# A hybrid attention layer on one core: two stores in place of four for each projected q and k, and a reordered preparation of the output projection's weights

## The chip, the cores and the metric

The kernel runs on one core of one Trainium2 chip. Its time is device time in microseconds for one execution of the whole layer; the figure quoted is the median of three runs. The core has a matrix engine (TensorE; PE in the profile, its weight loads PEld), three other compute engines (VectorE = DVE, ScalarE = ACT, GpSimd = POOL) and SyncE (SP), whose queue here issues nearly all transfers between the on-chip memory and DRAM (DMAs). Each engine works through its own instructions in order; semaphores hold an engine until what it needs from another is there.

## The reference

One layer, 1024 positions, width 1024, float32. All matrices are dense.

```python
h = x @ w_in                                    # 1024 x 5120
qa, ka, va, qb, kb, vb, ga, gb = split(h)       # 8 + 8 heads of 64, two gates of 1024
y_a = chunk_band_attention(qa, ka, va, rel_bias) @ w_proj_a     # softmax, band of 9 chunks of 64
y_b = stick_breaking_attention(qb, kb, vb) @ w_proj_b           # causal, cumulative log sums
mix = (sigmoid(ga + b) * y_a + sigmoid(gb + b) * y_b) @ w_out
x = layer_norm(alpha * x + mix, g1, b1)
g, u = split(x @ w_ffn_in)                      # 2 x 2816
x = layer_norm(alpha * x + (silu(g) * u) @ w_ffn_out, g2, b2)
```

## The kernel before

**Numbers and products.** Every operand of a matmul is split in two rounded halves: `split(hi, lo, src)` casts on ScalarE (hi) and subtracts on VectorE (lo = src - hi). A product is then three matmuls (hi·hi, hi·lo, lo·hi). Most big products use seven block products instead of eight (a Strassen-like scheme, numbered p1 to p7 and run in the order 1, 2, 6, 5, 7 or 3, ...); their weights and inputs are sums of blocks, made on VectorE beforehand. One block product is 12 matmuls of 128x512 in the input projection and in the feed-forward part, 24 in the output projection.

**Stages, in order of time.** (1) Input projection. The list `work` has entries 0 to 13: entry 0 is a pair of q and k columns made with plain products, entries 1 to 4 and 6 to 8 are further pairs of q and k by seven products, entry 5 is v, entries 9 to 13 are gates. `run_pairs` drives them; `left(i)` and `right(i)` load and split the weights of entry i (tiles wLp, wRp; the split sums are wlp, wbp, wap, wcp, here with the entry's number behind them: wap1 belongs to entry 1). Results are gathered in tiles called c, one for q and one for k: ScalarE copies a block product out of PSUM or VectorE adds it. `out_qk` then splits c into hi and lo, and `store_hl` stores both to DRAM (`q_dr`, `k_dr`), from which the heads load them later. An aside of this stage (`sum_wo`) makes sums of the blocks of `w_out` and stores them (`wt_dr`); another stores the split weights of the branch projections (`wp_dr`). (2) Eight softmax heads (tiles with _a), then eight stick-breaking heads (_b), with gate products and branch A's projection between them. (3) Branch B's projection: eight column blocks c, each two accumulators `yBps`, whose results are multiplied by the gate tile gB and added to the stored other branch (`mA`). (4) The output projection. Rows 0 to 511 use seven products, `ops` p1 to p7, with weight tiles "11", "21", "22" and the sums "t1" to "t4" (raw wr_o/wr_ot, halves wh_ and wl_); rows 512 to 1023 use plain products in a last loop over `hf` and `tt` with "11", "21", "12", "22". `take_in` adds a finished accumulator to the residual tile `acc`; `layer_norm` follows per 128 rows. (5) Feed-forward up and down, second layer norm.

**Slots and banks.** On-chip tiles come from rings of slots of 128x1024 floats by tag:

```python
SLOTS = dict(bw=9, pt=4, yt=3, qs=2, kh=2, kl=2, v=2, gt=3, kp=4, op=8, xt=16)
BANKS = dict(mm=2, sc=2, tr=3, pv=1)
```

In stage 1 the tiles c, hi and lo of the q/k pairs, the output tiles of v (vc) and the tiles of `sum_wo` and `store_proj` take turns in the eight slots of `QKV = ("qs", "kh", "kl", "v")` (`cycle`); entry 0's halves and some others use `("qs", "kl")` only. A new tile waits until the last reader of its slot is done; for a tile that was stored, that is the landing of its store. PSUM accumulators likewise come in rings of 2, 2, 3 and 1 banks.

**What sets the order.** The framework schedules instructions by itself; `tc.keep_in_program_order(ins)` ties an instruction to the order in which the code is written. SP's queue issues DMAs in its own order, and an issue waits there until its source is ready and its destination free; all that stands behind it on SP waits too. Eight DMA semaphores take turns, so a DMA also waits for the one issued eight places earlier on its semaphore to land.

**The part of the change.** `begin_w(srcs, name, raw, hl, lo_eng)` loads a weight tile and returns `end`, which makes its halves, the lower one on the engine `lo_eng`. Before, `begin_wo` gives GpSimd for "11", "21", "t1" to "t4" and VectorE for "22" and "12". A weight tile is begun when the one before has been ended, one or two products ahead of its use.

Of the kernel before, what the change touches and what calls it, by code (L numbers as in the profile page):

```python
# [11 lines left out]
F32 = mybir.dt.float32  # L12
# [6 lines left out]
P = 128  # L19
# [29 lines left out]
def hybrid_trunk_kernel(ctx: ExitStack, tc, x, xt, w_first, w_v, w_in, b_gate, rel_bias, w_proj,  # L49
# [272 lines left out]
    def small_inputs():  # L322

        rel_sb = cycle(QKV, "rel_sb")[0:8, 0:896]
        rel_in = cycle(QKV, "rel_in")[0:8, 0:N_REL]
        dma(rel_in, rel_bias)
        nc.vector.tensor_copy(rel_sb[:, 383:896], rel_in[:, ::-1])
        nc.vector.tensor_copy(rel_sb[:, 0:383], rel_in[:, 512:513].to_broadcast([8, 383]))
        dma(rel_dr, rel_sb)
        dma(bg, b_gate)  # L330

    def store_hl(d, hi, lo):
        for h in range(2):
            rows = slice(h * DH, (h + 1) * DH)
            dma(d[h * P:h * P + DH], hi[rows].bitcast(F32))
            dma(d[h * P + DH:(h + 1) * P], lo[rows])

    def project_plain(i):

# [162 lines left out]
    def aside_work(i):  # L502
        if i == 2:
            small_inputs()
        if i >= len(work) - 9:
            store_proj(i - len(work) + 9)
        if i in (5, 8):
            sum_wo(i // 6)

    def run_pairs(steps, left, right, also=lambda i: None, first=2, aside=lambda i: None,  # L510
                  then=lambda: None, wide=None, then_right=None):
# [24 lines left out]
            also(i)  # L536


    def begin_w(srcs, name, raw, hl, lo_eng):
        r = raw(f"wr_{name}")  # L540
        srcs = srcs if isinstance(srcs, list) else [(slice(0, 1024), srcs)]
        for cs, src in srcs:
            dma(r[:, cs], src)

        def end(tied=False):
            hi = hl(f"wh_{name}", F32R)
            lo = hl(f"wl_{name}", F32R)
            for ins in (nc.scalar.copy(hi, r),
                        lo_eng.tensor_tensor(lo, r, hi.bitcast(F32), ALU.subtract)):
# [419 lines left out]
    for hd in heads:  # L969
        for g in range(2):  # L970
# [7 lines left out]
            for st in range(8 - 4 * g):  # L978
                vsteps.append((hd, g, st, box))

    wi = 0
    pend = []
    steps_of = {}
# [6 lines left out]
    for si, (hd, g, st, box) in enumerate(vsteps):  # L990
        hidx, pos = si // nhead, si % nhead
        if hidx < 14 and pos == 8:
            load_qk(heads[hidx + 2])
            if hidx < 6:
                later.append([3, heads[hidx + 2]["end_bias"]])
        if pos == 4:
            if hidx < 15:
                load_v(heads[hidx + 1])
            else:
                next_w = begin_proj(1, 3)()  # L1000
        early = hd["br"] == 0 and st == LAG - 1 and len(pend) == LAG
# [70 lines left out]
    wo, m_raw = {}, {}  # L1072

    def begin_wo(name, raw, tag, lo_eng):
        ends = [begin_w((wt_dr if name in wt_dr else wo_src)[name][j], f"o{name}_{j}", of(raw),
                        of(tag), lo_eng) for j in range(2)]

        def end():
            wo[name] = [end_j() for end_j in ends]
        return end  # L1080

    def wo_op(name, kt):
        cs = (LO, HI)[kt % 2]
        return tuple(t[:, cs] for t in wo[name][kt // 2])

    for n, c in enumerate((6, 7, 5, 4, 0, 1, 2, 3)):
        if n % 2 == 0:
            w = next_w
            if n < 6:
                next_w = begin_proj(1, (2, 0, 1)[n // 2])()  # L1090
        gB = slot("kp", f"gB{c}")
        dma(gB, g_dr[2 * c + 1])
        squash(gB, c, 1)
        if c in kept:
            mA = kept[c]
        else:
            mA = slot("op", f"mA{c}")
            dma(mA, m_dr[c])
        for hf, cs in enumerate((LO, HI)):
            acc = bank("sc", f"yBps{c}_{hf}")  # L1100
            mm3(acc, [(w[0][:, ks], w[1][:, ks], yh[4 + k][:, cs], yl[4 + k][:, cs])
                      for k, ks in ((k, slice((c % 2) * HW + k * P, (c % 2) * HW + (k + 1) * P))
                                    for k in range(4))])
            nc.vector.tensor_tensor(gB[:, cs], acc, gB[:, cs], ALU.mult)
            nc.vector.tensor_tensor(mA[:, cs], gB[:, cs], mA[:, cs], ALU.add)
        m_raw[c] = mA
        t = m_high[c] = cycle(QKV, f"mo{c}", F32R)
        split(t[:, LO], t[:, HI], mA[:, HI])
        if c < 4:
            m_sums(c, m_raw[c + 4], mA)  # L1110
        else:
            g = m_first[c - 4]
            split(g[:, quarter(0)], g[:, quarter(1)], mA[:, quarter(0)])
        if n in (0, 3):
            wo_end = begin_wo(("11", "21")[n // 3], "pt", "xt", nc.gpsimd)
        elif n in (2, 5):
            wo_end()
        elif n == 6:
            more_acc("pt")
            more_acc("pt")  # L1120
    wo_end = begin_wo("t2", "gt", "op", nc.gpsimd)
    wo_end()
    wo_end = begin_wo("t1", "gt", "op", nc.gpsimd)


    def bcast(src, t):
# [171 lines left out]
            pieces.pop(0)()  # L1298

    def take_in(tt, cs, acc, scale=ALPHA):  # L1300
        nc.vector.scalar_tensor_tensor(acc_t[tt][:, cs], acc_t[tt][:, cs], scale, acc,
                                       ALU.mult, ALU.add)

    def norm_1(tt, quick):
        layer_norm(acc_t[tt], g1, b1, f"1_{tt}", quick)
# [3 lines left out]
    for p in (1, 2, 6, 5, 3, 7, 4):  # L1309
        first = p in (1, 2, 5)  # L1310
        name = {1: "11", 2: "21", 3: "22", 4: "t4", 5: "t1", 6: "t2", 7: "t3"}[p]
        t0, cs, scale = {1: (0, LO, ALPHA), 2: (0, LO, 1.0), 6: (0, HI, ALPHA), 5: (2, HI, ALPHA),
                         3: (0, HI, 1.0), 7: (2, HI, 1.0), 4: (2, LO, ALPHA)}[p]
        for j in range(2):
            accs = by if p in (2, 5, 3) else bx
            if first:
                accs[j] = bank({1: "mm", 2: "sc", 5: "tr"}[p], f"ops{p}_{j}")
            for kt in range(4):
                lh, ll = (t[:, j * P:(j + 1) * P] for t in m_op(p, kt))
                wh, wl = wo_op(name, kt)  # L1320
                for n, (a, b) in enumerate(((lh, wh), (lh, wl), (ll, wh))):
                    mm(accs[j], a, b, start=(first and kt == n == 0), stop=(kt == 3 and n == 2),  # L1322
                       skip_group_check=True)
            take_in(t0 + j, cs, accs[j], scale)
            if p in (3, 4):
                norm_1(t0 + j, False)
        if p == 1:
            wo_end()
            wo_end = begin_wo("22", "gt", "xt", nc.vector)
        elif p == 2:  # L1330
            ops_22 = [slot("yt", f"m22{q}", F32R) for q in "hl"]
            split(*ops_22, raw_22)
            for _ in range(2):
                more_acc("pt")
            wo_end()
            wo_end = begin_wo("t3", "gt", "op", nc.gpsimd)
        elif p == 6:
            wo_end()
            wo_end = begin_wo("t4", "gt", "op", nc.gpsimd)
        elif p == 5:  # L1340
            wo_end()
            wo_end = begin_wo("12", "gt", "xt", nc.vector)
        elif p == 3:
            for tag in ("yt", "yt", "yt", "bw"):
                more_acc(tag)
        elif p == 7:
            wo_end()

    left_f(0)
    R0 = slot("gt", "wRf0")  # L1350
    dma(R0, w_ffn_in[NF])
    Wf[0]["hr"] = split_w(R0, "wrf0", "bw")
    left_f(1)
    right_f(1)
    for hf, cs in enumerate((LO, HI)):
        for tt in range(4, 8):
            acc = bank(("mm", "sc")[hf], f"ops{tt}_{hf}")
# [6 lines left out]
                                  *wo_op(f"{blk + 1}{hf + 1}", kt)))  # L1364
            mm3(acc, pairs)
            take_in(tt, cs, acc)
            if hf == 1:
                norm_1(tt, tt > 5)
                if tt == 4:
                    x1_operands(0, acc_t)  # L1370
# [182 lines left out]
```

## Time and profile before

| what | value |
|---|---|
| median of 3 runs | 1450.07 us (1449.14 to 1450.41) |
| profiled execution | 1448.3 us, of which 1446.5 us is the span that the profile shows |
| granted TensorE clock | 0.995 of full speed |
| busy time in the span | PE 1418.2, DVE 1048.7, ACT 687.3, POOL 305.0 us |
| HBM | 179.33 MB read, 92.30 MB written |
| stage boundaries on PE | entry 1 from 27.7, first softmax head 341.3, branch B's projection 651.2, output projection 698.9, its last loop 747.1 us |

Busy shares are means over stages. PE is busy nearly all the time, so only the stretches in which PE waits, and what could make it wait longer, bear on the time. "A <- B" in a row of waits reads: A was idle until B was done. In a row of a timeline the numbers are the start and the duration in us, then engine, line, operation, output and inputs.

### The profile page before, as it was taken

The numbers are of one execution on the slowest core, as the hardware profiler recorded it, in microseconds if no ns is written. First come the engines' busy times: TensorE is split into PE (matmuls) and PEld (weight loads), VectorE is DVE, ScalarE is ACT, GpSimd is POOL, SyncE is SP. The second block draws the span as 40 slices with busy tenths as digits, with TensorE's granted clock in tenths as the row PEclk, the third lists the DMA queues.
The fourth block names the chain that finished last, engine by engine and source line by source line (L and its number), as shares of the span: only waits on it lengthen the run. The fifth ranks groups of instructions, "written<-read, shape, count | busy, mean of one in ns | idle before, by whom it ended". The sixth has DMA issues, their size and how long they took to land.

```text
span 1446.5 us, 19146 instructions
## 1 busy us (share of the span) xinstructions
PE 1418.2 (98%) x6672; PEld 1173.3 (81%) x6672; DVE 1048.7 (72%) x1653; ACT 687.3 (48%) x1194; POOL 305.0 (21%) x331
## 2 busy tenths in 40 slices
PE   9999998999999999999989999999999999999997
PEld 7888886888888888887768888888888888888886
DVE  8857745565777788877976966776767755978757
ACT  6434433455888787864433633444444433221201
POOL 0000000002556788742272000000000000100016
PEclk9999999999999999999999999999999999999999
DMA  7475569789787479836561133344444457786502
GB/s 250 131 242 160 200 226 288 255 298 248 207 223 205 137 225 282 261 126 241 200 215 57 59 117 114 140 154 161 160 154 152 146 202 258 284 313 236 204 16 102
DMA packets 105999, 276.55 MB, mean 191 GB/s; under 512 B 11424, under 2 KB 27808, under 8 KB 105904
## 3 DMA queue, kind: packets, MB, share of 16 engines
q1 hardware_dynamic: 105904, 275.35, 58.0%
q8 instruction: 52, 0.85, 0.2%
q14 instruction: 43, 0.35, 0.1%
HBM read 179.33 MB, written 92.30 MB: 188 GB/s over the span
## 4 chain that ended last, share of the span: by engine, by line
PE 90%; DVE 3%; DMA 2%; ACT 2%; issue 1%; POOL 1%; SPq 0%; POOLq 0%; DVEq 0%; ACTq 0%
PE sxf L180 16%; PE sxp L180 9%; PE szf L180 8%; PE dx L1475 6%; PE v L483 5%; PE szp L180 4%; PE gps L597 4%; PE syf L180 4%; PE dz L1475 3%; PE yAps L894 3%; PE syp L180 2%; PE tp_b L805 2%; PE tp_a L805 2%; PE ops L1322 2%; PE dy L1475 2%; PE plain L349 1%
## 5 line engine op out<-in xcount | busy, mean ns | idle before, releaser
L1431 POOL TENSOR_TENSOR wdyt<-wdyt 128x512 f32<-128x512 f32 x8 | 11.2, 1394 | 512.5 <-DMA x<-x_dr 422.8
L782 POOL TENSOR_TENSOR w_b<-w_b,kp_b 128x511 f32<-128x511 f32 (+3 forms) x96 | 96.2, 1013 | 30.7 <-DVE kp_b L777 21.4
L777 DVE TENSOR_TENSOR_SCAN kp_b<-kp_b,ident_ps 128x512 f32<-128x512 f32 (+2 forms) x64 | 56.6, 885 | 23.3 <-ACT kp_b L774 22.6
L717 POOL MEMSET bias<- 64x64 f32 x2 | 0.3, 144 | 323.2 <-ACT bias L713 323.2
L774 ACT ACTIVATE kp_b<-sc_b 128x512 f32<-128x512 f32 (+3 forms) x96 | 48.4, 504 | 30.8 <-PE sc_b L694 23.1
L180 PE MATMUL szf<-x1S63h,wcf 128*128 128x512 f32 x168 | 55.1, 389 | 0.0
L747 POOL TENSOR_SCALAR w_a<-w_a,st_a 128x640 f32<-128x640 f32 (+2 forms) x64 | 42.5, 669 | 59.4 <-DVE st_a L746 22.9
L111 DVE TENSOR_TENSOR pt_b<-tp_b,pt_b 128x512 fp32r<-128x512 f32 (+1 forms) x96 | 50.0, 544 | 6.9 <-ACT pt_b L110 6.3
L1406 DVE TENSOR_TENSOR x<-dx,x 128x512 f32<-128x512 f32 x64 | 43.4, 686 | 14.9 <-PE dx L1475 14.9
L111 DVE TENSOR_TENSOR sl<-h,sl 128x512 fp32r<-128x512 f32 x56 | 38.4, 685 | 18.8 <-ACT sl L110 18.8
L110 ACT CAST pt_b<-tp_b 128x512 fp32r<-128x512 f32 (+1 forms) x96 | 47.4, 504 | 8.1 <-PE tp_b L805 7.6
L742 ACT ACTIVATE w_a<-w_a,st_a 128x640 f32<-128x640 f32 (+2 forms) x64 | 44.8, 701 | 12.8 <-DVE st_a L736 10.8
L110 ACT CAST sl<-h 128x512 fp32r<-128x512 f32 x56 | 34.7, 619 | 33.4 <-PE syf L180 17.1
L1256 ACT ACTIVATE h<-sxf 128x512 f32<-128x512 f32 x21 | 12.5, 598 | 77.8 <-PE sxf L180 77.8
L805 PE MATMUL tp_b<-ident,w_b 128*128 128x128 f32 x288 | 47.8, 273 | 0.7 <-DVE pt_b L111 0.7
L775 ACT ACTIVATE w_b<-sc_b 128x511 f32<-128x511 f32 (+3 forms) x96 | 48.4, 504 | 0.0
L111 DVE TENSOR_TENSOR pt_a<-tp_a,pt_a 128x512 fp32r<-128x512 f32 (+1 forms) x96 | 44.8, 485 | 4.5 <-ACT pt_a L110 3.0
L1138 POOL TENSOR_TENSOR mv<-mv,neghalf 128x1 f32<-128x1 f32 x16 | 23.9, 1495 | 111.9 <-DVE mv L1137 111.9
L110 ACT CAST pt_a<-tp_a 128x512 fp32r<-128x512 f32 (+1 forms) x96 | 39.0, 432 | 11.5 <-PE tp_a L805 11.0
L805 PEld LDWEIGHTS tp_b<-ident,w_b 128*128 128x128 f32 x288 | 35.6, 140 | 10.0 <-PE sc_b L694 1.7
L805 PE MATMUL tp_a<-ident,w_a 128*128 128x128 f32 x240 | 43.1, 275 | 0.5 <-DVE pt_a L111 0.4
L597 PE MATMUL gps<-xl,wh_g 128*128 128x512 f32 x96 | 42.9, 447 | 0.0
(1790 smaller groups left out, 4871.6 us busy)
## 6 DMA issues: line engine op xcount, KB each, us to landing
s_dr<-sl SPq DMA_DIRECT2D x112, 256.0 KB, 2.3
sd<-s_dr SPq DMA_DIRECT2D x56, 512.0 KB, 4.6
wLf<-in_w_ffn_in_dram SPq DMA_DIRECT2D x22, 512.0 KB, 4.4
wRf<-in_w_ffn_in_dram SPq DMA_DIRECT2D x22, 512.0 KB, 3.7
v_dr<-vc SPq DMA_DIRECT2D x16, 512.0 KB, 3.1
qs<-q_dr SPq DMA_DIRECT2D x16, 512.0 KB, 6.8
kh<-k_dr SPq DMA_DIRECT2D x32, 256.0 KB, 6.5
kl<-k_dr SPq DMA_DIRECT2D x32, 256.0 KB, 6.2
```

The source lines that it names most:

```text
L110: return (nc.scalar.copy(dst_h, src), nc.vector.tensor_tensor(dst_l, src, dst_h.bitcast(F32), ALU.subtract))
L111: nc.vector.tensor_tensor(dst_l, src, dst_h.bitcast(F32), ALU.subtract))
L180: mm(acc, lw[:, ks], rx, start=(first and kt == i == 0), stop=(kt == 3 and i == 2), skip_group_check=not first)
L483: mm(accs[j], a, b, start=(first and kt == n == 0), stop=(kt == 3 and n == 2), skip_group_check=True)
L597: mm(acc[hf], lw[:, ks], rx[k][:, (LO, HI)[hf]], start=(k == j == 0), stop=(k == KT - 1 and j == 2))
L742: nc.scalar.activation(s[:, 0:w], s[:, 0:w], AF.Exp, bias=st[:, m:m + 1], scale=-1.0, accum_out=st[:, 2:3])
L774: nc.scalar.activation(kp[:, c0:e], sc[:, 0:n], AF.Sigmoid, scale=-1.0)
L775: nc.scalar.activation(be[:, m0:e], sc[:, m0 - c0:n], AF.Sigmoid)
L777: nc.vector.tensor_tensor_scan(kp[:, 0:e], kp[:, 0:e], ident_ps()[:, 0:e], 0.0, ALU.mult, ALU.add)
L782: nc.gpsimd.tensor_tensor(be[:, m0:e], be[:, m0:e], kp[:, m0 - 1:e - 1], ALU.mult)
L805: tr(tp[:, (qb - lo_q) * P:(qb - lo_q + 1) * P], wt[qb - q0][:, (kb - qb) * P:(kb - qb + 1) * P], ident)
L1475: mm(acc, a, b, start=(first and i == n == 0), stop=(i == n - 1 == 1), skip_group_check=not first)
```

## The change

1. `store_hl` stores a tile of 128 rows (two heads of 64) with one DMA in place of two: four DMAs of 64x1024 for the two halves become two, whose DRAM side is the pattern 2 x 64 x 1024. There were 64 such stores, now 32.
2. `sum_wo` runs at entries 2 and 6 instead of 5 and 8.
3. The lower halves of all output-projection weights are made on VectorE; cast and subtraction, the loads and `take_in` are tied in program order.
4. The tiles "11" and "21" are loaded during the last head into the slots of q, k and v, and "11" is ended before branch B's projection; the other raw tiles use slots of gt and bw.
5. Branch B's projection uses four PSUM banks (sc and mm in turn) instead of two, takes its blocks in the order 6, 7, 5, 4, 2, 3, 1, 0, and defers the split of the upper half (`high`).
6. The first weights of the feed-forward part (`left_f(0)`, `wRf0`, `left_f(1)`, `right_f(1)`) move from ahead of the last loop into it, behind its first accumulator; "12" is ended just ahead of that loop.

```diff
     def store_hl(d, hi, lo):
-        for h in range(2):
-            rows = slice(h * DH, (h + 1) * DH)
-            dma(d[h * P:h * P + DH], hi[rows].bitcast(F32))
-            dma(d[h * P + DH:(h + 1) * P], lo[rows])
+        parts = d.rearrange("(h n p) c -> n h p c", h=2, n=2)
+        for n, t in enumerate((hi.bitcast(F32), lo)):
+            dma(parts[n], t)
...
     def aside_work(i):
         if i == 2:
             small_inputs()
+        if i in (2, 6):
+            sum_wo(i // 6)
         if i >= len(work) - 9:
             store_proj(i - len(work) + 9)
-        if i in (5, 8):
-            sum_wo(i // 6)
...
+    def begin_wo(name, raws, tag):
+        ends = [begin_w((wt_dr if name in wt_dr else wo_src)[name][j], f"o{name}_{j}", of(raw),
+                        of(tag), nc.vector, True) for j, raw in enumerate(raws)]
+
+        def end():
+            wo[name] = [end_j(True) for end_j in ends]
+        return end
...
-    for n, c in enumerate((6, 7, 5, 4, 0, 1, 2, 3)):
+    for n, c in enumerate((6, 7, 5, 4, 2, 3, 1, 0)):
...
-            acc = bank("sc", f"yBps{c}_{hf}")
+            acc = bank(("sc", "mm")[hf], f"yBps{c}_{hf}")
...
     def take_in(tt, cs, acc, scale=ALPHA):
-        nc.vector.scalar_tensor_tensor(acc_t[tt][:, cs], acc_t[tt][:, cs], scale, acc,
-                                       ALU.mult, ALU.add)
+        t = acc_t[tt][:, cs]
+        tc.keep_in_program_order(nc.vector.scalar_tensor_tensor(t, t, scale, acc, ALU.mult, ALU.add))
...
-        elif p == 7:
-            wo_end()
-
-    left_f(0)
-    R0 = slot("gt", "wRf0")
-    dma(R0, w_ffn_in[NF])
-    Wf[0]["hr"] = split_w(R0, "wrf0", "bw")
-    left_f(1)
-    right_f(1)
+            end_12 = begin_wo("12", ("gt", "gt"), "xt")
+
+    end_12()
...
+            if hf == 0 and tt == 4:
+                left_f(0)
+                R0 = slot("gt", "wRf0")
+                dma(R0, w_ffn_in[NF])
+                Wf[0]["hr"] = split_w(R0, "wrf0", "bw")
+                left_f(1)
+                right_f(1)
```

**SP, entries 1 and 2 of the input projection.** Before, from the last store of entry 0 to the v weights (hi and c are entry 1's halves, q_dr and k_dr the DRAM tensors, wLp and wRp weight loads):

```order
L336 DMA k_dr_85<-lo_0_490 64x1024 x2
L629 DMA wLp_686<-in_w_in_dram 128x1024
L142 DMA wRp_701<-in_w_in_dram 128x1024
L131 DMA wLp_788<-in_w_in_dram 128x1024
L335 DMA q_dr_78<-hi_1_753 64x1024
L335 DMA k_dr_86<-hi_1_733 64x1024 x2
L336 DMA q_dr_78<-c_1_541 64x1024
L336 DMA k_dr_86<-c_1_651 64x1024 x2
L335 DMA q_dr_78<-hi_1_753 64x1024
L336 DMA q_dr_78<-c_1_541 64x1024
L142 DMA wRp_861<-in_w_in_dram 128x1024
```

The same stretch of SP now:

```order
L335 DMA k_dr_85<-lo_0_488 2x64x1024
L630 DMA wLp_682<-in_w_in_dram 128x1024
L142 DMA wRp_697<-in_w_in_dram 128x1024
L131 DMA wLp_780<-in_w_in_dram 128x1024
L335 DMA q_dr_78<-hi_1_747 2x64x1024
L335 DMA k_dr_86<-hi_1_729 2x64x1024
L335 DMA q_dr_78<-c_1_537 2x64x1024
L142 DMA wRp_849<-in_w_in_dram 128x1024
L335 DMA k_dr_86<-c_1_647 2x64x1024
```

Each pair of 64x1024 stores has become one of 2x64x1024; the weight loads stand between the stores as before.

**ACT, entry 1 of the input projection.** Before (wap1h and s24h are operands of entry 1's products, c_2 and c_3 the copies of the first products of entries 2 and 3):

```order
L110 CAST wbp1h<-tbp_513 128x1024
L110 CAST wcp_636<-wRp_477 128x512
L110 CAST s24h_226<-s_3_521 128x1024
L110 CAST wap1h<-tap_512 128x1024
L199 COPY c_2_570<-sxp_557 128x512
L199 COPY c_3_599<-sxp_586 128x512
```

Now:

```order
L110 CAST wbp1h<-tbp_509 128x1024
L110 CAST wcp_632<-wRp_477 128x512
L199 COPY c_2_566<-sxp_553 128x512
L110 CAST wap1h<-tap_508 128x1024
L110 CAST s24h_226<-s_3_517 128x1024
L199 COPY c_3_595<-sxp_582 128x512
```

The copy of entry 2's first product now stands ahead of two casts that entry 1 needs; its tile takes a slot of entry 0's lower halves.

**DVE, end of the seven products.** Before, from product 7 to product 4 (acc_7472 and acc_7474 are the residual tiles of rows 256 to 511, wl_o the lower halves of "12", bn/mv the norm of rows 0 to 255):

```order
L1139 SCALAR_TENSOR_TENSOR acc_7326<-acc_7326,mv_0_7580,ln1g 128x1024
L1301 SCALAR_TENSOR_TENSOR acc_7328<-acc_7328,ops_1_7540 128x512
L549 TENSOR_TENSOR wl_o_0_7649<-wr_o_0_7562,wh_o_0_7648 128x1024
L1135 BN_STATS bn_1_7603<-acc_7328 128x6
L549 TENSOR_TENSOR wl_o_1_7653<-wr_o_1_7564,wh_o_1_7652 128x1024
L1136 BN_AGGR mv_1_7604<-bn_1_7603 128x2
L1301 SCALAR_TENSOR_TENSOR acc_7472<-acc_7472,ops_0_7400 128x512
```

Now:

```order
L1315 SCALAR_TENSOR_TENSOR acc_7458<-acc_7458,ops_1_7383 128x512
L111 TENSOR_TENSOR wrf0l<-wRf_7704,wrf0h 128x1024
L1148 BN_STATS bn_3_7653<-acc_7458 128x6
L1149 BN_AGGR mv_3_7654<-bn_3_7653 128x2
L1150 TENSOR_SCALAR mv_3_7654<-mv_3_7654 128x1
L1152 SCALAR_TENSOR_TENSOR acc_7458<-acc_7458,mv_3_7654,ln1g 128x1024
L550 TENSOR_TENSOR wl_o_0_7665<-wr_o_0_7586,wh_o_0_7664 128x1024
L550 TENSOR_TENSOR wl_o_1_7669<-wr_o_1_7588,wh_o_1_7668 128x1024
L1315 SCALAR_TENSOR_TENSOR acc_7578<-acc_7578,ops_0_7672 128x512
```

The lower halves of "12" have moved from ahead of product 7's result to behind the norms of all four row blocks, just ahead of the last loop's first result (acc_7578).

More of the change, by code (lines that the diff above doesn't have):

```diff
@@ L536, in run_pairs, with begin_w @@
             also(i)
-    def begin_w(srcs, name, raw, hl, lo_eng):
+    def begin_w(srcs, name, raw, hl, lo_eng, in_turn=False):
         r = raw(f"wr_{name}")
@@ L542, in begin_w @@
         for cs, src in srcs:
-            dma(r[:, cs], src)
+            ins = dma(r[:, cs], src)
+            if in_turn:
+                tc.keep_in_program_order(ins)
         def end(tied=False):
@@ L979, in hybrid_trunk_kernel, with wo_op @@
                 vsteps.append((hd, g, st, box))
+    wo = {}
+    def begin_wo(name, raws, tag):
[4 more added lines that the diff above has]
+        return end
+    def wo_op(name, kt):
+        cs = (LO, HI)[kt % 2]
+        return tuple(t[:, cs] for t in wo[name][kt // 2])
     wi = 0
@@ L1000, in hybrid_trunk_kernel @@
                 next_w = begin_proj(1, 3)()
+                end_11, end_21 = (begin_wo(name, raws, "xt")
+                                  for name, raws in (("11", ("qs", "kh")), ("21", ("kl", "v"))))
+        if hidx == 15 and pos == 10:
+            end_11()
         early = hd["br"] == 0 and st == LAG - 1 and len(pend) == LAG
@@ L1070, in m_op, with high @@
         return o[kt][:, quarter(q)], o[kt][:, quarter(q + 2)]
[L1072 to L1084, printed above, removed]
-    for n, c in enumerate((6, 7, 5, 4, 0, 1, 2, 3)):
+    m_raw = {}
+    def high(c):
+        t = m_high[c] = cycle(QKV, f"mo{c}", F32R)
+        split(t[:, LO], t[:, HI], m_raw[c][:, HI])
+    for n, c in enumerate((6, 7, 5, 4, 2, 3, 1, 0)):
         if n % 2 == 0:
@@ L1089, in hybrid_trunk_kernel @@
             if n < 6:
-                next_w = begin_proj(1, (2, 0, 1)[n // 2])()
+                next_w = begin_proj(1, (2, 1, 0)[n // 2])()
         gB = slot("kp", f"gB{c}")
@@ L1106, in hybrid_trunk_kernel @@
         m_raw[c] = mA
-        t = m_high[c] = cycle(QKV, f"mo{c}", F32R)
-        split(t[:, LO], t[:, HI], mA[:, HI])
         if c < 4:
             m_sums(c, m_raw[c + 4], mA)
+            if n > 4:
+                high(last_c)
+            last_c = c
         else:
@@ L1113, in hybrid_trunk_kernel @@
             split(g[:, quarter(0)], g[:, quarter(1)], mA[:, quarter(0)])
-        if n in (0, 3):
-            wo_end = begin_wo(("11", "21")[n // 3], "pt", "xt", nc.gpsimd)
-        elif n in (2, 5):
-            wo_end()
-        elif n == 6:
+            high(c)
+        if n == 0:
+            end_21()
+        elif n == 3:
             more_acc("pt")
             more_acc("pt")
-    wo_end = begin_wo("t2", "gt", "op", nc.gpsimd)
-    wo_end()
-    wo_end = begin_wo("t1", "gt", "op", nc.gpsimd)
+        elif n == 6:
+            end_t2 = begin_wo("t2", ("gt", "gt"), "op")
+    end_t2()
+    end_t1 = begin_wo("t1", ("gt", "bw"), "op")
+    end_22 = begin_wo("22", ("gt", "gt"), "xt")
     def bcast(src, t):
@@ L1327, in hybrid_trunk_kernel @@
         if p == 1:
-            wo_end()
-            wo_end = begin_wo("22", "gt", "xt", nc.vector)
+            high(last_c)
+            end_t1()
+            end_t3 = begin_wo("t3", ("gt", "bw"), "op")
         elif p == 2:
+            end_22()
+            end_t4 = begin_wo("t4", ("gt", "gt"), "op")
             ops_22 = [slot("yt", f"m22{q}", F32R) for q in "hl"]
@@ L1334, in hybrid_trunk_kernel @@
                 more_acc("pt")
-            wo_end()
-            wo_end = begin_wo("t3", "gt", "op", nc.gpsimd)
         elif p == 6:
-            wo_end()
-            wo_end = begin_wo("t4", "gt", "op", nc.gpsimd)
+            end_t3()
         elif p == 5:
-            wo_end()
-            wo_end = begin_wo("12", "gt", "xt", nc.vector)
+            end_t4()
         elif p == 3:
```

1 line of the change is left out of this document (removed).

## The prediction

> **What bounds the kernel now.** I read the page first: engine shares, the chain that ended last, the DMA line.
>
> ```profile
> PE 1418.2 (98%) x6672; PEld 1173.3 (81%) x6672; DVE 1048.7 (72%) x1653; ACT 687.3 (48%) x1194; POOL 305.0 (21%) x331
> PE 90%; DVE 3%; DMA 2%; ACT 2%; issue 1%; POOL 1%; SPq 0%; POOLq 0%; DVEq 0%; ACTq 0%
> DMA packets 105999, 276.55 MB, mean 191 GB/s; under 512 B 11424, under 2 KB 27808, under 8 KB 105904
> ```
>
> PE is 90% of the chain and the change leaves its 6672 matmuls alone. So the time can fall only by what PE waits, and rise by whatever makes PE wait longer. The waits of PE:
>
> ```profile
> PE ops L1322 <- DVE mv L1137: 7.1, 1, 7.1
> PE sxp L180 <- ACT wbp9h L110: 4.9, 1, 4.9
> PE yBps L117 <- DVE gB L1104: 3.0, 4, 1.2
> PE ops L1322 <- DVE acc L1301: 0.9, 1, 0.9
> ```
>
> These are what the edits can win: 15.9 us, 11.0 of them in branch B's and the output projection, and some 5 us of slow matmuls right behind the waits (shown below). Then the transfers, because the change gives the q and k stores another shape (table of issues, and the tile q_dr):
>
> ```profile
> q_dr<-hi SPq DMA_DIRECT2D x16, 256.0 KB, 3.9
> x_dr<-acc SPq DMA_DIRECT2D x8, 512.0 KB, 2.6
> rel_dr<-rel_sb SPq DMA_DIRECT2D x1, 28.0 KB
> rel_in<-in_rel_bias_dram SPq DMA_DIRECT2D x1, 16.0 KB
> ...
> who waited for it (us, times):
>   ACT c L212: 3.5, 2
>   ACT c L199: 1.7, 1
> ```
>
> A store of 256 KB lands in 3.9 us, and already ScalarE's copies into c wait 5.2 us for slots that a q store still holds. The two transfers of 8 rows have no landing time.
>
> **The stores: how many DMA engines carry one.** The counts in the table of issues add up to 707 transfers. If each closes with one small packet on each of 16 engines, that is 11312, and the gate bias adds 128 packets of 64 B: 11440. The page counts 11424, 16 fewer. The two 8-row transfers explain exactly that if each used 8 engines instead of 16. Their rows of 2052 and 3584 B could have been cut finer to feed all 16 and weren't: a transfer is dealt out in whole steps of its outermost dimension. The old stores had 64 steps. The new one is written 2 x 64 x 1024: two steps. No row of this trace has an outermost 2, so the price lies between 16 engines (a store as x_dr's, 2.6 us) and 2. I take 2, the reading that the 8-row transfers are nearest to.
>
> The Trainium skill, "DMA: Bandwidth & Descriptors", section "Why a DMA increments its semaphore by 16 and not by 1", speaks against the change: the number of engines is the largest up to 16 that divides the slowest dimension of both sides as the instruction carries it, and on this kind of queue they are the lowest-numbered ones. By that rule each new store runs on the same two engines, where a reading by rows would give 16 and the time of the first rival below; the trace agrees with it at 8 rows and shows nothing at 2. By the page's rate, about 27 GiB/s for an engine, a store would take 9.0 us (an estimate), which makes the sum below some 50 us smaller.
>
> What does an engine move? In the first loads all 16 were full:
>
> ```profile
> 12.00:20.00 8.00, 8.00 (x37) 6.64 (x36) 7.97 (x14) 6.67 (x11) 0.00 (x0) 1.00 1.04 397
> 60.00:250.00 190.00, 185.04 (x810) 151.40 (x809) 115.00 (x134) 79.08 (x103) 0.00 (x0) 1.00 0.68 219
> ```
>
> 397 GB/s over 16 is 24.8 GB/s, so 262144 B on each of two engines take 10.6 us; the projection's mean, 219 GB/s over 0.68 x 16, is 20.1 GB/s and 13.0 us. I take 10.6, since two engines have the memory nearly to themselves. Any 512 KB transfer over 16 engines costs each 1.3 us, also those two. All go through SP's one queue, so I count a load as served behind the stores issued before it.
>
> **The ledger of those two engines**, on the changed kernel's clock. The rows it hangs on (timeline, chain, tile sc_a), all of before:
>
> ```profile
> 23.36 1.16 SPq L335 DMA_DIRECT2D q_dr<-hi  x2
> 57.66 0.39 PE L180 MATMUL sxp<-s24h,wbp2h 128*128 128x512 f32 x1
> 147.89 0.39 PE L483 MATMUL v<-vh,s13h 128*128 128x512 f32 x1
> 180.53 0.39 PE L180 MATMUL sxp<-xh,wlp6h 128*128 128x512 f32 x1
> 235.39 5.44 PE sxp L180 x24
> L693 PE MATMUL sc_a<-kh,qs x96: 221/309/485, 341.3 to 458.8; 128*128 128x320 f32 x64, 128*128 128x512 f32 x8, 128*128 128x384 f32 x8, 128*128 128x256 f32 x8
> ```
>
> They give the first store's issue, the end of entry 1, v's fifth pass (p7), the start of entry 6, a product (12 matmuls, 2.72 us) and the start of the heads.
>
> 1. Entry 0: data start 1.3 us after the issue (2.6 less 1.3). 24.7 + 4 x 10.6 + 2 loads x 1.3 = 69.7, landed at 70.5.
> 2. Entry 1: the copy into c of entry 2 needs the slot of entry 0's last store, and behind that copy ScalarE holds the casts wap1h and s24h, without which entry 1's last 4 1/4 products (11.6 us) can't run. They end near 84.5 instead of 57.66; stores from 88.
> 3. Entries 1 to 3: 12 stores and 7 loads without a gap, 88 + 127.2 + 9.1 = 224.
> 4. Entry 4's first copy needs the slot of entry 3's last store. 38 matmuls (8.6 us), a cast and a subtraction later, near 239, its first half is ready; sum_wo's eight transfers and four v weights, which now lie here, hold the engines to 243. Stores to 286.
> 5. v: the weights of p7 queue behind them and land at 288; with their sum and split, p7 starts near 291 instead of 147.89, 143 late. The rest of v takes 32.6, so entry 6 starts at 324.
> 6. Entries 6 and 7: six products and 4 us for the halves bring the first store to 344. 8 stores and 7 others: 345.5 + 94 = 439.5.
> 7. Entry 8: its first copy waits for entry 7's third store (428); 12 other transfers (15.6) come first, then four stores, to 498.
> 8. Entry 10's first copy needs the slot of entry 8's last store, 499. Six products (16.3) bring entry 11 to 515; the 21 products of entries 11 to 13 (57.1) bring the heads to **572 instead of 341.3: +231 us**. The wait for wbp9h disappears inside this.
>
> By the heads' start these two queues are empty again; what follows is as before but for the other edits.
>
> **Branch B's projection and the output projection.** Rows, of before:
>
> ```profile
> L549 POOL TENSOR_TENSOR wl_ot<-wr_ot,wh_ot 128x1024 fp32r<-128x1024 f32 x8 | 20.5, 2583 | 38.8 <-ACT wh_ot L548 35.9 <-DVE mb L111 2.8
> L1147 POOL TENSOR_TENSOR acc<-acc,ln1b 128x1024 f32<-128x1024 f32 x6 | 16.0, 2669 | 7.6 <-ACT acc L1146 7.6
> L1138 POOL TENSOR_TENSOR mv<-mv,neghalf 128x1 f32<-128x1 f32 x8 | 12.0, 1503 | 30.0 <-DVE mv L1137 30.0
> L549 DVE TENSOR_TENSOR wl_o<-wr_o,wh_o x4: 1211/1634/2535, 717.5 to 736.7; 128x1024 fp32r<-128x1024 f32 x4
> ...
> 724.91 8.11 POOL L549 TENSOR_TENSOR wl_ot<-wr_ot,wh_ot 128x1024 fp32r<-128x1024 f32 x3
> 727.33 3.69 SPq L543 DMA_DIRECT2D wr_o<-in_w_out_dram  x2
> 736.68 2.54 DVE L549 TENSOR_TENSOR wl_o<-wr_o,wh_o 128x1024 fp32r<-128x1024 f32 x1 [1.97 <-ACT wh_o L548]
> 739.26 0.63 DVE L1301 SCALAR_TENSOR_TENSOR acc<-acc,ops 128x512 f32<-128x512 f32 x1
> 740.03 0.77 PE L1322 MATMUL ops<-wh_ot,m22h 128*128 128x512 f32 x1 [7.06 <-DVE mv L1137]
> 747.13 0.39 PE L117 MATMUL ops<-wh_o,mo 128*128 128x512 f32 x1
> ```
>
> The 7.1 us wait: GpSimd's lower halves (2.6 us each, three in a row to 733.0) keep the gt slots; the raw "12" so lands late, VectorE waits for it at 736.68, and product 7's result, which PE needs, stands behind, at 739.26. Now "12" stands behind the norms, and that wait goes. With it goes what follows: product 4's 24 matmuls took 7.1 us (740.03 to 747.13) instead of two products' 5.44, for PE runs slowly at first after a long wait. Twelve lower halves more on VectorE cost 12 x 1.2 = 14.5 us there; but the same subtraction took 1.21 us alone and 2.54 beside GpSimd, and 1.3 saved at each of the twelve is 15.6. A wash, bounded by -2 and +4 on PE, since VectorE is seldom last. Four banks give an eviction two accumulators (5.4 us) more time where the longest wait was 1.2, so the 3.0 and the 0.9 go too. 7.1 + 1.7 + 3.0 + 0.9, and 1.6 for the slow matmuls behind the short waits: -14.3, by which the last loop begins at 732.8 instead of 747.13. What is late next is "12" itself: four norms in a row take 1.5 + 2.7 us on GpSimd and about 1.1 on ScalarE each, from 721, where product 3 is taken in, to 742; the casts of "12" stand behind them on ScalarE, its lower halves end near 744, and PE wants the first result's bank, two accumulators into the loop, at 743.7: about 0.9 lost. `wRf1` then takes the slot that frees, lands some 4 us later, and its sums stand ahead of the second result: about 2.0 more. In all **-11.4 us**, bounds -15 and -6. `sum_wo`'s move costs nothing of its own; it lies within steps 4 and 7.
>
> **Sum.** The profiled execution took 1448.3 us: At five places of the ledger (steps 2, 4, 5, 7, 8) PE starts on the path after a long wait, at 1.7 us each: +8. 1448.3 + 231 + 8 - 11.4 = 1675.9; the median of the runs lies 1.8 above the profiled execution: **1678 us**. Low end: loads don't queue behind stores (41 x 1.3 = 53 less) and the gaps shrink by 15: 1610. High end: 13.0 us a store, 32 x 2.4 = 77 more: 1755.
>
> **Rivals.**
> - *The new store spreads over 16 engines.* It costs less than the two it replaces (2.6 against 2 x 3.9), SP issues 32 fewer, and the wait for wbp9h (4.9, with the slow matmuls behind it 6.8) goes: `wRp9` now stands ahead of entry 7's stores. 1448.3 - 6.8 - 11.4 = 1430, median 1432, faster. For it: 64-row stores did use 16. Against: the missing 16 packets.
> - *Two engines, but other ones each time.* A store then lands in about 10.6 + 1.3 = 12 us instead of 4, yet nothing queues behind it. Only the copies into c that already wait feel it, 8 us at some two to four places: +16 to +32 less 18, so 1448 to 1464; about 1455. It decides against the first rival as soon as two such copies stand ahead of PE. Against it: nothing in the trace shows engines taking turns.
> - *VectorE becomes last in the output projection.* Lower halves in order ahead of `take_in`: if the 15.6 us saved don't come, PE waits up to +4 where I count -11.4. Too small to turn any of the other cases.
>
> **Chances.** Two fixed engines 0.86, sixteen 0.09, two rotating ones 0.05. The range 1610 to 1755 holds about 0.93 of the first case, 0.80 in all; it is that case's own range. A measurement here can tell 0.2% (2.9 us) from no change. Faster: 0.09 and a little of the third case, 0.10; within 0.2%: 0.02; slower: 0.88.
>
> **What would show it.** Page: 675 transfers close with 675 x 16 + 128 - 16 = 10912 small packets if sixteen engines carry the stores, with 14 x 32 = 448 fewer, about 10464, if two. Table of issues: q_dr and k_dr stores landing in 12 us and up to 45, loads in between as late. DMA share between 25 and 500 us near 0.2 instead of 0.6. PE waits for ACT's c, wRp and wv; the first sc_a near 572. At the end, no PE wait for mv, and a new one of 1 to 2 us each at the first two results of the last loop. I am wrong in the mechanism if those stores land under 5 us, and in the size if they land in 12 but entry 4 starts before 200 us.

## The result and the profile after

| | median (us) | runs from - to | ratio to before, 95% interval |
|---|---|---|---|
| before, same chip | 1450.24 | 1449.14 - 1451.07 | |
| changed kernel | 1678.1 | 1676.83 - 1678.69 | 1.1571, 1.1551 to 1.1591 |

The changed kernel is 15.7% slower; the forecast was 1678 (1610 to 1755). The profiled execution took 1678.51 us, of which 1676.7 is the span. The page of after: engine shares, DMA line, chain.

```profile
PE 1441.1 (86%) x6672; PEld 1189.8 (71%) x6672; DVE 1050.7 (63%) x1665; ACT 687.4 (41%) x1194; POOL 272.9 (16%) x319
DMA packets 105041, 276.57 MB, mean 165 GB/s; under 512 B 10464, under 2 KB 26848, under 8 KB 104944
PE 68%; DMA 16%; issue 7%; DVE 3%; ACT 2%; SPq 2%; POOL 1%; POOLq 0%; DVEq 0%; ACTq 0%
```

DMA has gone from 2% to 16% of the chain, and the small packets are 10464, the number worked out for stores on two engines. The same matmuls keep PE busy 22.9 us longer (1441.1 against 1418.2), which no wait explains; that is taken up below. Busy time by stage, before (to the heads, then the two attention parts, branch B's projection, the output projection):

```profile
0.00:341.30 341.30, 334.82 (x1449) 273.20 (x1450) 218.14 (x268) 157.31 (x208) 1.30 (x11) 0.99 0.70 230
341.30:651.20 309.90, 307.26 (x1778) 260.06 (x1776) 247.15 (x578) 244.03 (x588) 205.25 (x271) 1.00 0.73 209
651.20:699.00 47.80, 44.81 (x194) 35.74 (x193) 38.60 (x62) 21.38 (x33) 11.28 (x5) 1.00 0.61 220
699.00:795.00 96.00, 87.86 (x394) 71.70 (x393) 75.15 (x96) 36.79 (x46) 45.90 (x21) 0.96 0.47 159
```

The same stages after; the columns are length, busy PE, PEld, DVE, ACT, POOL, then granted clock, DMA share, GB/s:

```profile
0.00:577.70 577.70, 356.55 (x1449) 288.28 (x1450) 219.71 (x268) 157.94 (x208) 1.31 (x11) 0.80 0.38 137
577.70:886.50 308.80, 307.26 (x1778) 260.07 (x1776) 247.15 (x578) 245.09 (x590) 205.55 (x271) 1.00 0.74 215
886.50:930.10 43.60, 43.60 (x194) 36.06 (x193) 38.63 (x67) 20.64 (x34) 0.00 (x0) 1.00 0.59 206
930.10:1024.70 94.60, 89.80 (x394) 72.73 (x393) 75.35 (x103) 35.97 (x45) 24.79 (x13) 0.96 0.46 156
```

All of the loss lies ahead of the heads: 577.7 - 341.3 = +236.4 us, of which 21.7 is PE busy longer and 214.7 PE idle. From there to the end the kernel is 6.2 us shorter: 1.1 in the attention parts, 4.2 in branch B's projection, 1.4 in the output projection, less 0.5 in the rest. What the idle time waits for shows on ScalarE (waits of ACT, 25 to 520 us):

```profile
ACT c L199 <- DMA q_dr<-c: 45.5, 1, 45.5
...
ACT vc L492 <- DMA q_dr<-hi: 26.9, 1, 26.9
ACT c L199 <- DMA k_dr<-lo: 26.4, 1, 26.4
ACT c L208 <- DMA q_dr<-c: 26.0, 1, 26.0
ACT c L199 <- DMA q_dr<-hi: 23.4, 1, 23.4
```

Copies out of PSUM wait for the slot of a tile whose store has not landed, and PE waits for them (waits of PE, the whole run):

```profile
PE sxp L180 <- ACT c L199: 98.6, 3, 44.1
PE sxp L180 <- DVE c L195: 34.0, 1, 34.0
PE sxp L180 <- ACT c L208: 31.9, 2, 25.9
PE szp L180 <- DVE c L195: 20.4, 1, 20.4
PE v L482 <- ACT vc L492: 11.9, 1, 11.9
PE sxp L180 <- ACT s24h L110: 11.8, 1, 11.8
PE sxp L180 <- DVE lo L365: 10.2, 1, 10.2
```

These are ten waits of 6.0 to 44.1 us, 218.8 us in all. What the stores do meanwhile is seen where nothing else runs (windows of after, then of the timeline of SP):

```profile
180.00:205.00 25.00, 0.00 (x0) 0.00 (x0) 0.00 (x0) 0.00 (x0) 0.00 (x0) 0.50 0.13 53
```

```profile
92.35 7.09 SPq L335 DMA_DIRECT2D q_dr<-c  x1
99.49 9.70 SPq L142 DMA_DIRECT2D wRp<-in_w_in_dram  x1
109.29 1.02 SPq L335 DMA_DIRECT2D k_dr<-c  x1
110.36 9.74 SPq L326 DMA_DIRECT2D rel_in<-in_rel_bias_dram  x1
```

For 25 us no engine works and the DMA share is 0.13: two of sixteen, at 53 GB/s. SP's issues stretch too: a load's issue, 0.3 us elsewhere, takes 9.70 us behind queued stores. One store per 9.7 us is 262144 B / 9.7 us = 27.0 GB/s for each of the two engines; the 53 GB/s of the window above are 26.5 for each.

### The profile page after: what moved, and what is told of

It reads as the page before. It is cut to its first block, busy times and chain, and to the rows that moved or that the text cites. A ratio compares the mean times of both kernels' runs of the same rounds, so it can differ in the third digit from the quotient of the medians.

```text
span 1676.7 us, 19118 instructions
## 1 busy us (share of the span) xinstructions
PE 1441.1 (86%) x6672; PEld 1189.8 (71%) x6672; DVE 1050.7 (63%) x1665; ACT 687.4 (41%) x1194; POOL 272.9 (16%) x319
## 2 busy tenths in 40 slices
DMA packets 105041, 276.57 MB, mean 165 GB/s; under 512 B 10464, under 2 KB 26848, under 8 KB 104944
## 4 chain that ended last, share of the span: by engine, by line
PE 68%; DMA 16%; issue 7%; DVE 3%; ACT 2%; SPq 2%; POOL 1%; POOLq 0%; DVEq 0%; ACTq 0%
PE sxf L180 13%; PE szf L180 7%; PE sxp L180 6%; DMA q_dr<-c 6%; PE dx L1488 5%; DMA q_dr<-hi 4%; PE gps L598 4%; PE syf L180 3%; PE v L482 3%; PE szp L180 3%; PE dz L1488 3%; DMA wo22r<-in_w_out_dram 2%; PE yAps L895 2%; PE tp_a L806 2%; PE tp_b L806 2%
## 5 line engine op out<-in xcount | busy, mean ns | idle before, releaser
L195 DVE TENSOR_TENSOR c<-syp,c 128x512 f32<-128x512 f32 x12 | 8.3, 689 | 91.7 <-ACT c L199 83.7
L151 DVE TENSOR_TENSOR tap<-wRp,wLp 128x512 f32<-128x512 f32 x12 | 8.3, 688 | 69.9 <-DMA wRp<-in_w_in_dram 69.9
L806 PE MATMUL tp_b<-ident,w_b 128*128 128x128 f32 x288 | 47.8, 273 | 0.4 <-DVE pt_b L111 0.3
L199 ACT COPY c<-sxp 128x512 f32<-128x512 f32 x12 | 7.0, 586 | 97.8 <-DMA q_dr<-c 45.5
```

The source lines that it names most:

```text
L806: tr(tp[:, (qb - lo_q) * P:(qb - lo_q + 1) * P], wt[qb - q0][:, (kb - qb) * P:(kb - qb + 1) * P], ident)
```

## The experiments

Each was timed beside the kernel before on the same chip; there before was at 1449.1 (first four), 1449.2 (E5 to E7) and 1449.9 (E8 to E10).

**E1 (e1_old_stores): the 64-row stores back, all other edits kept.**

```diff
-        parts = d.rearrange("(h n p) c -> n h p c", h=2, n=2)
-        for n, t in enumerate((hi.bitcast(F32), lo)):
-            dma(parts[n], t)
+        for h in range(2):
+            rows = slice(h * DH, (h + 1) * DH)
+            dma(d[h * P:h * P + DH], hi[rows].bitcast(F32))
+            dma(d[h * P + DH:(h + 1) * P], lo[rows])
```

> The changed kernel with the 64 stores of 64 rows of the kernel before; all its other edits stay. If the two-engine stores are the whole loss: 1437 us (1430 to 1445), that is 1450.2 less 6.8 for the wait for wbp9h and the slow matmuls behind it and less the 6.2 that the later stages have gained; first sc_a near 335. If the moved sum_wo or the tied order in the output projection carry part of the loss, the time lies that much above 1450.

1445.75 us, ratio 0.9971 (0.9959 to 0.9983). The loss is gone with the stores. But the time is 8.75 above the expectation, and the first sc_a (the start of the heads) is at 345.8, not 335. PE's waits ahead of the heads:

```profile
PE v L483 <- ACT vh L110: 2.5, 1, 2.5
PE sxp L180 <- DVE c L195: 1.9, 1, 1.9
PE sxp L180 <- ACT c L208: 1.4, 1, 1.4
PE v L483 <- DVE vl L111: 1.3, 2, 0.7
```

The wait for `wbp9h` is gone as expected, and others, in v and entry 8, are new. E10 takes this up.

**E2 (e2_only_merge): the merged stores alone, on the kernel before** (the edit of change 1).

> The kernel before with store_hl of the changed kernel as its only edit. If the two-engine stores are the whole loss: 1678.1 plus the 6.2 that the later stages no longer gain, 1684 us (1665 to 1705), first sc_a 560 to 600, about 10464 small packets. If the loss hangs on the other edits: within 10 us of 1450.

1672.74 us, ratio 1.1542 (1.1521 to 1.1563), 10464 small packets, first sc_a at 564.6: the merged stores are the loss. The rest of the change is no help on top of it: E2 is 5.4 below the changed kernel. By the spans (1670.4 against 1676.7) its heads start 13.1 earlier (564.6 against 577.7) and the part from there takes 6.8 longer. Ahead of the heads the two differ in the place of `sum_wo`.

**E3 (e3_rows): one store for 128 rows, but with 128 outer steps.**

```diff
-        parts = d.rearrange("(h n p) c -> n h p c", h=2, n=2)
         for n, t in enumerate((hi.bitcast(F32), lo)):
-            dma(parts[n], t)
+            dma(d[n * P:(n + 1) * P], t)
...
-        q, k = (d[i][h * P:(h + 1) * P] for d in (q_dr, k_dr))
+        q, k = (d[i].rearrange("(n h p) c -> n h p c", n=2, h=2)[:, h] for d in (q_dr, k_dr))
...
-                dma(t.bitcast(F32), q)
+                for half, row in ((slice(0, DH), q[0]), (slice(DH, P), q[1])):
+                    dma(t[half].bitcast(F32), row)
...
-                    dma(t[half].bitcast(F32), k[part:part + DH])
+                    dma(t[half].bitcast(F32), k[part // DH])
```

> The changed kernel with q_dr and k_dr laid out as upper halves of both heads, then lower halves, so that a store is 128x1024: still one DMA for 128 rows, but 128 outer steps. The heads load q by two DMAs of 64 rows instead of one, 16 more transfers. If the outermost dimension sets the number of engines: as the kernel with 64-row stores, 1437 us (1428 to 1445), 691 x 16 + 128 - 16 = 11168 small packets. If a store of 256 KB in one DMA is slow whatever its shape: 1678 as the changed kernel.

1437.39 us, ratio 0.9920 (0.9908 to 0.9933). The same bytes in the same number of stores now land in medians of 2.7 to 4.0 us (issues of E3, the last column; two of the four groups) and cost nothing:

```profile
DMA packets 105743, 276.55 MB, mean 193 GB/s; under 512 B 11168, under 2 KB 27552, under 8 KB 105648
...
q_dr<-hi SPq DMA_DIRECT2D x8, 512.0 KB, 2.8
...
q_dr<-c SPq DMA_DIRECT2D x7, 512.0 KB, 4.0
```

PE waits for nothing over 0.3 us between entry 1 and the heads, which start at 332.9: 8.4 earlier than before and 12.9 earlier than in E1. Merging the stores is a good edit; the order of the dimensions was the fault.

**E4 (e4_four): four outer steps.** `q_dr` and `k_dr` in blocks of 32 rows, so that a store is 4 x 32 x 1024 (loads of 32 rows to match).

```diff
-            dma(parts[n], t)
+            dma(d.rearrange("(b n r) c -> n b r c", b=4, n=2)[n], t)
```

> The changed kernel with q_dr and k_dr laid out in blocks of 32 rows, upper and lower halves in turn, so that a store is 4x32x1024: the same bytes in the same number of stores, outermost 4. The heads load by pieces of 32 rows, 112 more transfers. If the outermost dimension is the number of engines: 5.3 us a store on each of four; the ledger run with that loses some 56 us ahead of the heads where it lost 212 with two, so first sc_a near 398 (375 to 425), about 1500 us (1475 to 1530), and 787 x 16 + 112 - 32 x 12 = 12320 small packets. If stores of more than two dimensions are always on two engines: 1678 or more, 12256 small packets. If only the kind of pattern were slow and not the number of engines: no time between the two.

1650.91 us, ratio 1.1392 (1.1371 to 1.1412). The number of engines is as expected: 12321 small packets, and, where stores run alone, a share of 0.25 and 99 GB/s, four of sixteen:

```profile
DMA packets 106897, 276.57 MB, mean 168 GB/s; under 512 B 12321, under 2 KB 28705, under 8 KB 106801
```

```profile
130.00:135.00 5.00, 0.00 (x0) 0.00 (x0) 0.00 (x0) 0.00 (x0) 0.00 (x0) 0.75 0.25 99
0.00:443.50 443.50, 349.79 (x1447) 283.26 (x1448) 219.95 (x268) 158.15 (x208) 1.31 (x11) 0.89 0.49 174
```

The time was missed twice. The heads start at 443.8 instead of 398: the ledger gave a loss of some 56 us for all of that part, and ScalarE's c and vc alone waited 71 us for stores of q and k to land. And the heads and what follows up to branch B's projection take 414.8 us instead of 309. They hold the 112 extra loads, but that these cost the 106 us is not shown: PE is busy 53 us longer there (359.9 against 307.3, at a granted clock of 0.92) and idle 53 us longer, in many waits of at most 3.0 us for GpSimd, ScalarE and VectorE, and in none for a load. The start of the heads is what this run can tell: 332.9, 443.8 and 577.7 for 16, 4 and 2 engines.

**E5 (e5_sum_late): E3 with `sum_wo` at entries 5 and 8 again.**

```diff
-        if i in (2, 6):
-            sum_wo(i // 6)
...
+        if i in (5, 8):
+            sum_wo(i // 6)
```

> The kernel with 128x1024 stores (e3_rows), but sum_wo at entries 5 and 8 again. If the move of sum_wo costs and gains nothing by itself when no store queues: 1437.4 as e3_rows, within 2 us. If it is the move that took away the wait for wbp9h: that wait and its slow matmuls come back, 6.8 more, 1444. If the move costs ScalarE and VectorE work ahead of v (as the waits for vh and vl in e1_old_stores suggest, 4 us there): 2 to 4 us less than e3_rows.

1435.67 us, ratio 0.9902 (0.9889 to 0.9916): within 2 us of E3, and the heads start at 332.7 against 332.9. With these stores the place of `sum_wo` is free, and the wait for `wbp9h` stays away in both places.

**E7 (e7_rows_only): the stores of E3 as the only edit on the kernel before.**

> The kernel before with the 128x1024 stores and the row layout of e3_rows as its only edit. If the edits of branch B's and the output projection are worth the 6.2 us that they gained in the changed kernel, and nothing else: 1437.4 + 6.2 = 1443.6 (1442 to 1446). If sum_wo's move is needed to take away the wait for wbp9h: 1450. If those edits are worth the 11.4 of the forecast and the rest was lost elsewhere: 1449.

1444.8 us, ratio 0.9965 (0.9951 to 0.9979), first sc_a at 333.1. Against E3 and E5 the edits of branch B's and the output projection are worth 7.4 and 9.1 us.

**E10 (e10_old_late): E1 with `sum_wo` at entries 5 and 8**, so that only branch B's and the output projection differ from before.

> The kernel with the 64-row stores and all other edits (e1_old_stores), but sum_wo at entries 5 and 8 again, so that it differs from the kernel before in branch B's and the output projection alone. If those edits gain what they gained in the changed kernel: 1449.2 - 6.2 to 7.5 = 1442.5 (1441 to 1444.5), first sc_a 341. If sum_wo's early place is free with 64-row stores too: 1445.8 as e1_old_stores.

1443.12 us, ratio 0.9953 (0.9937 to 0.9968), first sc_a at 341.9, and the old wait is back:

```profile
PE sxp L180 <- ACT wbp9h L110: 4.9, 1, 4.9
```

So with 64-row stores the early `sum_wo` removes 4.9 us of wait and adds 7.1 (E1's four rows). The heads start 3.9 us later for it and the median is 2.6 us higher, though the intervals of E1's and E10's ratios still overlap (0.9959 to 0.9968). What removes the wait for good is the merged store on sixteen engines (E3, E5, E7); whether by the smaller number of DMAs or by their quicker landing was not separated.

**E6 (e6_both) and E8 (e8_tail): the two waits left in the output projection.** In the changed kernel and in E3 PE still waits twice there. Timeline of after, all engines, around the first of them:

```profile
958.59 1.27 DVE L1152 SCALAR_TENSOR_TENSOR acc<-acc,mv,ln1g 128x1024 f32<-128x1024 f32 x1
...
961.54 3.49 DVE L1152 SCALAR_TENSOR_TENSOR acc<-acc,mv,ln1g 128x1024 f32<-128x1024 f32 x1
961.56 2.39 POOL L1160 TENSOR_TENSOR acc<-acc,ln1b 128x1024 f32<-128x1024 f32 x1 [1.26 <-ACT acc L1159]
...
964.96 0.68 DVE L1315 SCALAR_TENSOR_TENSOR acc<-acc,ops 128x512 f32<-128x512 f32 x1
...
965.78 0.47 PE L1335 MATMUL ops<-wh_ot,m22h 128*128 128x512 f32 x1 [2.28 <-DVE acc L1315]
...
981.59 3.74 DVE L550 TENSOR_TENSOR wl_o<-wr_o,wh_o 128x1024 fp32r<-128x1024 f32 x2 [2.56 <-ACT wh_o L549]
985.25 0.67 DVE L1315 SCALAR_TENSOR_TENSOR acc<-acc,ops 128x512 f32<-128x512 f32 x1
985.98 0.50 PE L117 MATMUL ops<-wh_o,mo 128*128 128x512 f32 x1 [2.02 <-DVE acc L1315]
```

The norm's L1152 takes 1.27 us alone and 3.49 beside GpSimd's add: 2.39 of waiting and 1.1 of work. The Trainium skill, "SBUF — State Buffer", section "Who interferes with whom", describes such a lock for a VectorE instruction with two inputs in SBUF against a GpSimd instruction that reads SBUF. The trace agrees in that one of the two stands still while the other runs; which one is not to be told from the start times, since VectorE's, the one held up, is recorded 0.02 us earlier. The result that product 4 needs stands behind it. In the last loop the first result stands behind the halves of "12". E6 moves the norms of rows 0 to 255 behind product 7 and `end_12` to the same place, both on E3:

```diff
-            if p in (3, 4):
+            if p == 4:
                 norm_1(t0 + j, False)
...
+        elif p == 7:
+            for j in range(2):
+                norm_1(j, False)
+            end_12()
...
-    end_12()
```

> The kernel with 128x1024 stores (e3_rows) and two moves in the output projection: the norms of rows 0 to 255 stand behind product 7 instead of product 3, and the weight tile 12 is ended behind product 7 instead of ahead of the last loop. If the waits ahead of product 4 (2.5 us) and in the last loop (2.0) come from VectorE's instructions that stand there beside GpSimd's adds and behind the late casts of tile 12: both go, with 1.6 us of slow matmuls behind each, 1437.4 - 7.7 = 1429.7 (1428 to 1433). If PE only waits for the next of the norms' instructions instead: 1435 to 1438.

1436.35 us, ratio 0.9907 (0.9894 to 0.9921): the second theory. The norms' move worked (0.8 us left ahead of product 4), but the casts of "12" now stand on ScalarE behind a norm that waits for GpSimd, and product 4's own result behind its lower halves (E6, timeline):

```profile
727.50 1.15 ACT L1159 ACTIVATE acc<-acc,mv 128x1024 f32<-128x1024 f32 x1 [3.78 <-POOL mv L1151]
...
728.56 1.98 ACT L548 CAST wh_o<-wr_o 128x1024 fp32r<-128x1024 f32 x2
...
729.62 3.73 DVE L549 TENSOR_TENSOR wl_o<-wr_o,wh_o 128x1024 fp32r<-128x1024 f32 x2 [1.97 <-ACT wh_o L548]
...
733.27 0.68 DVE L1315 SCALAR_TENSOR_TENSOR acc<-acc,ops 128x512 f32<-128x512 f32 x1
```

E8 keeps the norms' move and puts "12" late instead, where its first use is still two accumulators away; `right_f(1)`, with the sums of `wRf1`, moves to behind the third accumulator:

```diff
-    end_12()
...
             if hf == 0 and tt == 4:
...
                 left_f(1)
+            if hf == 0 and tt == 5:
+                end_12()
+            if hf == 0 and tt == 6:
                 right_f(1)
```

> The kernel with 128x1024 stores (e3_rows) and three moves in the output projection: the norms of rows 0 to 255 behind product 7 instead of product 3; weight tile 12 ended behind the second accumulator of the last loop (it is first needed by the fifth) instead of ahead of the loop; the sums of wRf1 behind the third accumulator. If what PE still waits for there is VectorE's queue: the wait ahead of product 4 falls from 2.5 to 0.8 us as in e6_both, the one in the last loop (2.0 in e3_rows, 3.3 and 0.6 in e6_both) goes, and the slow matmuls behind both with them: 1437.4 - 6.9 = 1430.5 (1428.5 to 1433.5). If the wait only moves to the next result once more: 1435 to 1438.

1430.77 us, ratio 0.9874 (0.9857 to 0.9892), as expected. All that PE still waits for in the output projection (waits of E8, the one row with `ops`):

```profile
PE ops L1335 <- DVE acc L1315: 0.8, 1, 0.8
```

**E9 (e9_tail_late): E8 with `sum_wo` late.**

> As e8_tail, with sum_wo at entries 5 and 8 as in e5_sum_late. If its place costs nothing once no store queues: within 2 us of e8_tail.

1430.22 us, ratio 0.9869 (0.9851 to 0.9887), the same as E8. Both beat the kernel before by 1.3%.

## Why the prediction was right, point by point

**Two fixed engines: shown.** The packet count, the share of 0.13, E3 (16 engines, no loss) and E4 (4 engines, 12321 packets). The rule of the Trainium skill, "DMA: Bandwidth & Descriptors", section "Why a DMA increments its semaphore by 16 and not by 1", gave 2, 4 and 16 for the three layouts, and the runs agree with all three. The rival of other engines each time, with nothing queued behind a store, is out: with several stores issued its share would not stay at 0.13 for 25 us. Which two engines they are, no view here tells. Two of the signs came otherwise than written: the DMA share between 25 and 500 us is 0.32, not near 0.2 (0.70 before, from 25 to 341), and PE's long waits are for c, vc, s24h and lo, none for wRp or wv. The table of issues of this run has no landing times, so the pace of the issues stands in for them.

**The price of a store: too high.** I took 10.6 us; the issues behind full queues follow each other at 9.7, so the 9.0 us set beside it was too low. Over the 32 stores of the ledger that is up to 29 us too much. The ledger's steps, forecast and found:

| step | forecast (us) | found (us) |
|---|---|---|
| entry 1's stores from | 88 | 89.78 |
| entry 3's last store lands, PE goes on with entry 4 | 224 | 219.29 |
| entry 4's stores from | 243 | 232.21 |
| entry 6's first store | 344 | 339.95 |
| entry 8's last store lands, PE goes on in entry 10 | 499 | 504.80 |
| heads | 572, +8 | 577.7 |

The middle steps came 4 to 11 us early, as the lower price has it. The last ones are 6 late against steps that leave the +8 out; against 572 + 8 the heads came 2.3 us early. PE's slow stretches (next) are long enough to have taken up the lead.

**Slow matmuls after a wait: the term that was mis-sized.** I put 1.7 us at each of five places, +8. PE was busy 21.7 us longer ahead of the heads. The windows around the wait that ends at 168.80 show why:

```profile
165.00:170.00 5.00, 1.20 (x3) 1.04 (x4) 1.50 (x4) 1.31 (x2) 0.00 (x0) 0.50 0.34 126
170.00:175.00 5.00, 5.00 (x13) 3.69 (x12) 4.50 (x4) 3.15 (x4) 0.00 (x0) 0.54 0.13 53
...
225.00:230.00 5.00, 5.00 (x24) 4.14 (x23) 2.48 (x4) 1.06 (x1) 0.00 (x0) 1.00 0.44 177
```

Behind the wait the granted clock is 0.54 and 13 matmuls run in 5 us where 24 run at full clock. Over all ten long waits the first 5 us behind the wait hold 9 to 16 matmuls, 13 in the mean. Eleven matmuls of 0.21 us are 2.3 us for each wait, and there were ten of them, not five: 23, near the 21.7. So the forecast of the heads was close because of two errors that cancel: 16 us too much waiting (231 against 214.7), 14 too little slow running.

**Branch B's and the output projection: -11.4 came as -5.6** (-6.2 for all from the heads on). Branch B's part was right (47.8 to 43.6). The step that failed is "that wait goes. With it goes what follows": the wait for mv went, but VectorE's next instruction, the norm beside GpSimd's add, kept product 4 waiting 2.3 us, with 1.7 of slow matmuls behind. I had priced this very contention for the lower halves (1.21 against 2.54) and not for the norm that stays. The new stalls in the last loop came as one, of 2.0 us and 1.7 of slow matmuls, not as 0.9 and 2.0: the third accumulator needs the bank of the first result, which stands behind the halves of "12" and was taken in only from 985.25, some 2 us too late; `wRf1`'s sums held up nothing. E8 shows what both were worth: 6.6 us.

**`sum_wo`'s move "costs nothing of its own": wrong here, right in E5.** Its transfers stand in steps 4 and 7, but the ledger was not run for its old place. The heads start 13.1 us later for the move where stores queue (changed kernel against E2), and 3.9 later with 64-row stores (E1 against E10).

**The first rival, 1432, is in effect E3, at 1437.39.** The wait for `wbp9h` does go there, and the 5.4 us of difference are about what the output projection gained less than forecast.

**The sum.** On the span: forecast 1446.5 + 231 + 8 - 11.4 = 1674.1, found 1446.5 + 214.7 + 21.7 - 6.2 = 1676.7. That the total agrees within 0.1 us of the median is luck, since errors of some 15 us cancel in it; the mechanism is not.

## What to carry to other kernels

Before two DMAs become one, look at the outermost dimension of the new pattern: 2 steps put 512 KB on two engines (9.7 us), 4 on four, 128 on sixteen (2.7 to 4.0 us), and the same merge turns from +224 us to a gain of 4 (E2, E7). A transfer on few engines is seen in a DMA share that sits at 2/16 while nothing else runs, and it holds up all that stands behind it on its queue. Count with a wait of PE the slow matmuls behind it, here some 2.3 us for each of the ten long waits and 1.7 for those of 2.0 and 2.3 us, and when a wait is removed, ask what stands next in the same engine's order and beside whom it runs.

## What the runs showed of the hardware

- SP's issue itself is held: 9.7 us for a load on sixteen engines whose issue takes 0.33 us elsewhere, once stores on two engines are queued ahead. So loads do not just queue behind such stores, the issuing engine stands still.
- A wait of only 2.28 us (965.78) was enough for the clock to fall: 0.57 in the 4 us behind it, after 1.00 from 960.00 to 963.50. Product 4's 24 matmuls took 7.14 us (965.78 to 972.92) instead of 5.44. The row:

```profile
966.00:970.00 4.00, 4.00 (x12) 3.13 (x12) 1.97 (x3) 0.63 (x1) 2.38 (x1) 0.57 0.47 140
```
